# Forget-gate sums and step-width softplus issued beside projection steps in a hybrid streaming encoder step

## The chip, the cores and the metric

The kernel runs on one core of one Trainium2 chip. The metric is the device time of one execution in microseconds. The core has five engines that run side by side and wait for each other through semaphores: PE (matrix products), DVE (vector work), ACT (activation functions and copies), POOL (further element-wise work) and SP, which issues the DMAs here. PE writes to PSUM banks, and ACT or DVE must read a bank out before PE may fill it again.

## The reference

One layer of a trunk is computed for 1024 frames of a new stream and for 16 frames of each of 8 running streams, 1152 rows in all. Three mixers work on the same normalised input: a stick-breaking attention (4 heads), a forgetting attention "FoX" (4 heads) and a state-space scan "SSD" (8 heads). One input projection feeds all three.

```python
proj = jnp.einsum('bnd,de->bne', u, p['w_in'])
sq, sk, sv, fq, fk, fv, fg, z, xbc, dt = split_last(proj, IN_SIZES)
logf = jax.nn.log_sigmoid((fg + p['fox_b_f']).astype(jnp.float32))
fcum = jnp.cumsum(logf, axis=1)                      # running sum of the forget gates
fox_o = query_sweep(lambda qb, fb, qp: fox_attend(qb, fk, fv, fb, fcum, qp, kpos), (fq, fcum), n)
xbc_c = jax.nn.silu(causal_dwconv(xbc_pad, p['conv_w'], p['conv_b']))
dt = jax.nn.softplus((dt + p['dt_bias']).astype(jnp.float32))   # the step widths
y, h_final = ssd_scan(xs * dt[..., None], dt * A, Bm, Cm, h0, ssd_chunk)
```

For the running streams the sums of the gates start from 1024 cached gate values of each stream. After the mixers come an output projection, a cross-attention and a SwiGLU feed-forward net.

## The kernel before

All products are in split precision: an operand is stored as a rounded part (hi) and a remainder (lo), and each product is three matmuls (function `mm3`, lines L328 to L330). Weights are loaded by SP into `wr` tiles (4 buffers), ACT casts the hi part into `wh` (L292) and POOL subtracts to get the lo part `wl` (L132, in pieces of at most 256 columns). The same `wr`, `wh` and `wl` buffers also hold the cached keys and values of the running streams.

The middle of the program interleaves two generators. The **main** one is `pipeline`: 112 steps of attention, first the stick-breaking heads (`m = 0`), then the FoX heads (`m = 1`). A step is a block of 128 query rows (scores L561/L562, mask L564, then for `m = 0` two sigmoids on ACT L518/L519, a running product on DVE L521 and a product on POOL L132), or the product of finished weights with the values (transposes L579, ACT copies L582, products L594). In between are four decode units per mixer, each for two running streams: their rows load cached keys (L886), transpose them (L892, copies L894), and score them (L877, L905, L906); their value step is L928, L937 and L960.

The **fill** is a second generator, from which the loop takes one step per attention step (`RATE[0]` = 1.0). It is `fill_s`: projections of FoX queries and keys in 12 steps, of FoX values and gates in 9 (`proj_v(1)`; the gates go to tile `lf`), then `fox_sums` in 4 steps and `pad_cols`, then, in the order of `ORD`, the first half of z with the step widths in 9 steps (`z_proj(0)`; widths go to tile `dts`), `dt_softplus` in 1, the eight convolution blocks `xbc` in 24, and the second half of z in 9. A projection step is one output tile: 24 matmuls for a z block, in one PSUM bank of the pool `psd`, which has 2 banks. When `fill_s` ends, the SSD generator `ssd_gen` (51 steps) takes its place at 1.1 steps per attention step. What is left of it when attention ends runs between the steps of the output projection.

`fox_sums` and `dt_softplus` have no projection in them. Each turns gates into log form by a chain of small ACT and DVE instructions (`log1p_exp_negabs`, L402 to L412). `fox_sums` then makes running sums by small products (L686, L687, L694, L709 to L711, L729, each with a `psd` bank), scans (L700) and DMAs to and from DRAM. A z block's bank is read three times before it is free: by ACT for the tanh and by DVE for the gate (`gate`, L417 and L418) and for the step widths (L804).

The order on each engine is not written out: a scheduler places the instructions by their order of issue as priority and by its own model of time. Each engine then runs its queue strictly in that order, so an instruction that waits also holds up all behind it.

Of the kernel before, what the change touches and what calls it, by code (L numbers as in the profile page):

```python
# [62 lines left out]
def tile_hybrid_step(ctx: ExitStack, tc: tile.TileContext, a: dict):  # L63
# [34 lines left out]
    def xc_t(dt=F32):  # L98
        return xcp.tile([P, 1056], dt, tag="xc", name="xc")
# [10 lines left out]
    def pd():  # L110
        return ps_t(psd, "d")
# [230 lines left out]
    def dense_T(w, uc, jobs):  # L342


        units = [(w_unit([(w, c0, P)], 0, KT), f) for c0, f in jobs]
        for c in range(NCH):
            for (wh, wl), consume in units:
                ps = pd()
                uh, ul = uc[c]
                for k in range(KT):  # L350
                    mm3(ps[:, :CW], wh[:, k, :], wl[:, k, :], uh[:, k, :], ul[:, k, :], k == 0, k == KT - 1)
                later = consume(c, ps[:, :CW])
                flush()
                if later:
                    late.append(later)
                yield
# [4 lines left out]
    def flush():  # L361
        if late:
            late.pop()()

    def dense_N(srcs, ub, consume):

        n = sum(s[2] for s in srcs)
        u0 = w_unit(srcs, 0, 4)
        u1 = w_unit(srcs, 4, 4)
        for blk, (uh, ul) in enumerate(ub):  # L370
            ps = pd()
            for k in range(KT):
                wh, wl = (u0, u1)[k // 4]
                mm3(ps[:, :n], uh[:, k, :], ul[:, k, :], wh[:, k % 4, :], wl[:, k % 4, :],
                    k == 0, k == KT - 1)
            consume(blk, ps[:, :n])
            yield

    def blocks_of(uc):
        return [(uc[b // 3][0][:, :, (b % 3) * P:(b % 3 + 1) * P],  # L380
                 uc[b // 3][1][:, :, (b % 3) * P:(b % 3 + 1) * P]) for b in range(NBLK)]
# [38 lines left out]
    def drain(g):  # L420
        for _ in g:
            pass
# [361 lines left out]
    def pad_cols():  # L784
        sct = xc_t()[0:24, :D]
        SP.dma_start(out=sct, in_=a["state_conv"][0].rearrange("b i c -> (b i) c"))
        tp = pd()
        for j in range(8):
            PE.transpose(tp[:, 24 * j:24 * j + 24], sct[:, j * P:(j + 1) * P], ident[:24, :24])
        DVE.tensor_copy(pads, tp[:, :192].rearrange("p (j b i) -> p j b i", j=8, i=3))  # L790

    def xbc_proj(j0, j1):
        for j in range(j0, j1):
            yield from dense_T(w_in, uc, [xbc_job(j)])
        flush()


    def consume_z(n):
        def f(blk, ps):
            t, zt = sg2_t(), sg_t()  # L800
            gate(zt[:, :256], ps[:, :256], t, 0.5)
            SP.dma_start(out=z_sc[blk * P:(blk + 1) * P, n * 256:(n + 1) * 256], in_=zt[:, :256])
            if n == 0:
                DVE.tensor_tensor(out=dts[:, blk, :], in0=ps[:, 256:264], in1=hb[:, 4:12], op=ALU.add)  # L804
        return f

    def z_proj(n):
        yield from dense_N([(w_in, C_Z + 256 * n, 256)] + [(w_in, C_DT, 8)] * (n == 0), blocks_of(uc), consume_z(n))

    def dt_softplus():  # L810
        l = log1p_exp_negabs(dts, [P, NBLK, 8])
        DVE.scalar_tensor_tensor(dts.rearrange("p a b -> p (a b)"), dts.rearrange("p a b -> p (a b)"), 0.0,
                                 l.rearrange("p a b -> p (a b)"), ALU.max, ALU.add)
# [414 lines left out]
    aux = chunks((0, 1, 2))  # L1228
# [5 lines left out]
    drain(dense_T(w_in, uc, [(C_SK + P, consume_qk(3, 1, None, p_k[0], s_k[0]))]))  # L1234
    drain(proj_v(0, C_SV, p_v[0], s_v[0]))

    def fill_s():
        yield from dense_T(w_in, uc, [(C_FQ, consume_qk(4, 0, QS))])
        yield from dense_T(w_in, uc, [(C_FQ + P, consume_qk(5, 1, QS))])
        yield from dense_T(w_in, uc, [(C_FK, consume_qk(6, 0, None, p_k[1], s_k[1]))])  # L1240
        yield from dense_T(w_in, uc, [(C_FK + P, consume_qk(7, 1, None, p_k[1], s_k[1]))])
        yield from proj_v(1, C_FV, p_v[1], s_v[1], extra=4)
        yield from fox_sums()
        pad_cols()
        for o in ORD:
            if o == "z1":

                for hd in range(4):
                    tc.keep_in_program_order(
                        SP.dma_start(out=fs4.rearrange("(b h) i k -> b h i k", h=4)[:, hd],  # L1250
                                     in_=fs_sc[hd].unsqueeze(1).to_broadcast([DEC_B, 4, PAST])))
                for p in range(4):
                    tc.keep_in_program_order(
                        SP.dma_start(out=fqs[:, p:p + 1], in_=fn_sc[8 * p:8 * p + 8, :]))
            if o[0] == "z":
                yield from z_proj(int(o[1]))
            elif o == "dt":
                dt_softplus()
                yield
            else:  # L1260
                yield from xbc_proj(*o)

    def mixed(m, at, fc, nxt):

# [22 lines left out]
    u0, _ = mixed(0, AT0, None, load1)  # L1287
# [747 lines left out]
```

## Time and profile before

| | |
|---|---|
| time, median of 3 runs | 1906.57 us (1905.22 to 1914.69) |
| span of the profiled execution | 1911.2 us |
| its own time | not listed apart from the span |
| PE busy | 1834.5 us, 96% of the span |
| DVE, ACT, POOL busy | 894.3, 822.7, 627.9 us |

The profile is of one execution. Its span alone is 4.6 us above the median of the runs, 0.24%, so it stands among the slower ones. In the views, "x" is a count, a bracket gives the idle time before an instruction and what ended it, and PEclk is the clock that PE was granted, 1.00 being full speed. Matmuls overlap, so PE's busy time counts covered time. The profile calls L521 and L700 scans by their own name; the listings of the order call them SCALAR_TENSOR_TENSOR.

### The profile page before, as it was taken

The numbers are of one execution on the slowest core, as the hardware profiler recorded it, in microseconds if no ns is written. First come the engines' busy times: TensorE is split into PE (matmuls) and PEld (weight loads), VectorE is DVE, ScalarE is ACT, GpSimd is POOL, SyncE is SP. The second block draws the span as 40 slices with busy tenths as digits, with TensorE's granted clock in tenths as the row PEclk, the third lists the DMA queues.
The fourth block names the chain that finished last, engine by engine and source line by source line (L and its number), as shares of the span: only waits on it lengthen the run. The fifth ranks groups of instructions, "written<-read, shape, count | busy, mean of one in ns | idle before, by whom it ended". The sixth has DMA issues, their size and how long they took to land.

```text
span 1911.2 us, 32463 instructions
## 1 busy us (share of the span) xinstructions
PE 1834.5 (96%) x12120; PEld 1637.6 (86%) x12120; DVE 894.3 (47%) x1823; ACT 822.7 (43%) x1779; POOL 627.9 (33%) x923
## 2 busy tenths in 40 slices
PE   7989988999998899999999999999999999999998
PEld 5889876888876677899998889999999999788886
DVE  3421323557656882354444487333333333455554
ACT  6531543535666870344343275333333333344443
POOL 7632416254224662211112105454444542000000
PEclk9999998999999999999999999999999999999999
DMA  9455645536579896345567124223322223566672
GB/s 338 141 165 159 207 139 129 161 102 186 174 237 291 268 323 217 111 144 162 180 210 270 61 83 119 70 71 81 88 73 70 70 70 104 188 196 228 183 245 91
DMA packets 302365, 306.07 MB, mean 160 GB/s; under 512 B 82428, under 2 KB 253668, under 8 KB 302208
## 3 DMA queue, kind: packets, MB, share of 16 engines
q1 hardware_dynamic: 302208, 304.01, 51.4%
q8 instruction: 95, 1.56, 0.3%
q14 instruction: 62, 0.51, 0.1%
HBM read 229.84 MB, written 74.63 MB: 159 GB/s over the span
## 4 chain that ended last, share of the span: by engine, by line
PE 81%; DMA 6%; DVE 3%; POOL 3%; issue 3%; ACT 2%; SPq 1%; POOLq 0%; DVEq 0%; ACTq 0%
PE psd L1857 11%; PE psd L328 10%; PE psd L329 10%; PE psd L330 9%; PE pst L1857 8%; PE pss L1857 4%; PE pss L328 3%; PE pss L329 3%; PE pss L330 3%; PE pso L1857 2%; PE pso L594 2%; PE pst L328 1%; PE pst L329 1%; PE pst L330 1%; POOL wl L132 1%
## 5 line engine op out<-in xcount | busy, mean ns | idle before, releaser
L132 POOL TENSOR_TENSOR wl<-wr,wh 128x256 fp32r<-128x256 f32 (+2 forms) x184 | 140.9, 800 | 219.4 <-ACT wh L292 215.7
L328 PE MATMUL psd<-act,wh 128*128 128x384 f32 x576 | 199.2, 346 | 4.8 <-DVE sg L455 2.7
L329 PE MATMUL psd<-act,wh 128*128 128x384 f32 x576 | 197.9, 344 | 0.0
L330 PE MATMUL psd<-act,wl 128*128 128x384 f32 x576 | 197.1, 342 | 0.0
L1857 PE MATMUL pst<-bT,tr 128*128 128x256 f32 (+1 forms) x1068 | 155.0, 293 | 0.0
L1857 PEld LDWEIGHTS pst<-bT,tr 128*128 128x128 f32 x1068 | 144.9, 188 | 0.1
L328 PE MATMUL psd<-wh,act 128*128 128x256 f32 (+3 forms) x414 | 133.7, 326 | 3.4 <-DMA act<-osc 1.5
L330 PE MATMUL psd<-wh,act 128*128 128x512 f32 (+3 forms) x424 | 136.6, 323 | 0.0
L329 PE MATMUL psd<-wl,act 128*128 128x256 f32 (+3 forms) x414 | 133.7, 324 | 0.0
L1857 PE MATMUL psd<-bT,tr 128*128 128x320 f32 (+1 forms) x912 | 132.9, 295 | 0.8 <-DVE tr L1701 0.5
L1857 PEld LDWEIGHTS psd<-bT,tr 128*128 128x128 f32 x912 | 124.7, 188 | 1.3 <-DVE tr L1701 0.7
L328 PEld LDWEIGHTS psd<-act,wh 128*128 128x128 f32 x576 | 109.3, 190 | 8.4 <-DVE sg L455 3.1
L132 POOL TENSOR_TENSOR tr<-u,tr 128x256 fp32r<-128x256 f32 x110 | 82.6, 780 | 100.2 <-ACT tr L1697 82.2
L329 PEld LDWEIGHTS psd<-act,wh 128*128 128x128 f32 x576 | 109.5, 190 | 1.5 <-issue 1.1
L330 PEld LDWEIGHTS psd<-act,wl 128*128 128x128 f32 x576 | 109.2, 190 | 1.3 <-issue 1.0
L132 POOL TENSOR_TENSOR ws<-ws 128x256 f32<-128x256 f32 (+2 forms) x100 | 70.1, 729 | 115.1 <-DVE ws L521 102.4
L253 POOL TENSOR_SCALAR sm<-sm 128x1 f32<-128x1 f32 (+2 forms) x27 | 8.3, 308 | 299.0 <-ACT y L1940 210.7
L1832 DVE TENSOR_TENSOR tr<-tr,pst 128x256 f32<-128x256 f32 (+1 forms) x86 | 38.6, 449 | 138.3 <-ACT tr L1829 105.1
L132 POOL TENSOR_TENSOR tr<-raw,tr 128x256 fp32r<-128x256 f32 x94 | 69.4, 767 | 85.6 <-ACT tr L1697 77.5
L1697 ACT CAST tr<-tr 128x384 fp32r<-128x384 f32 (+1 forms) x70 | 37.7, 538 | 121.4 <-DMA tr<-hidsc 119.0
L328 PEld LDWEIGHTS psd<-wh,act 128*128 128x128 f32 x414 | 79.2, 192 | 11.6 <-issue 1.8
L292 ACT CAST wh<-wr 128x512 fp32r<-128x512 f32 (+2 forms) x90 | 52.2, 621 | 80.9 <-PE psd L330 31.0
(622 smaller groups left out, 4697.9 us busy)
## 6 DMA issues: line engine op xcount, KB each, us to landing
u<-w_down SPq DMA_DIRECT2D x40, 512.0 KB
raw<-w_down SPq DMA_DIRECT2D x26, 512.0 KB
st<-qksc SPq DMA_DIRECT2D x48, 256.0 KB
wr<-w_in SPq DMA_DIRECT2D x44, 256.0 KB
tr<-hidsc SPq DMA_DIRECT2D x57, 192.0 KB
hidsc<-tr SPq DMA_DIRECT2D x34, 288.0 KB
qksc<-sg SPq DMA_DIRECT2D x48, 192.0 KB
wr<-cache_sb_k SPq DMA_DIRECT2D x32, 256.0 KB
```

What stands on the lines that cost most here:

```text
L132: POOL.tensor_tensor(out=out[:, a0:a1], in0=in0[:, a0:a1], in1=in1[:, a0:a1], op=op)
L253: POOL.tensor_scalar(v, ss, inv, EPS, ALU.mult, ALU.add)
L292: ACT.copy(hi, raw)
L328: PE.matmul(out, ah, bh, start=start, stop=False)
L329: PE.matmul(out, ah, bl, start=False, stop=False)
L330: PE.matmul(out, al, bh, start=False, stop=stop)
L594: return PE.matmul(po[r:r + 64, q_], vt[:, 2 * (k0 + i) + j, :], pfs[i][:, sl], start=start and k0 == 0 and (j == 0 or qp > 0), stop=k0 + ...
L1697: ACT.copy(hi, src)
L1832: DVE.tensor_tensor(out=at(out, g), in0=at(x, g), in1=ps[g][:, :GW[g]], op=op)
L1857: PE.matmul(dst[g][:, :GW[g]], x[:, ka], y[:, k, :], start=start and k == 0 and m == 0, stop=stop and k == 3 and m == 2, skip_group_check= ...
```

## The change

The four steps of `fox_sums` and the one of `dt_softplus` no longer take a step of the fill. A helper `beside` draws one step of a second generator after each step of a projection, before the projection's step ends. `fox_sums` and `pad_cols` so run with the blocks 1 to 5 of `z_proj(0)`, and `dt_softplus` with the second tile of the first `xbc` block. The fill has 63 projection steps then, where it had 68 steps with 63 projections among them.

```diff
+    def beside(main, aux):
+        for _ in main:
+            next(aux, None)
+            yield
+        drain(aux)
+    def sums():
+        yield
+        yield from fox_sums()
+        pad_cols()
+    def steps():
+        yield
+        dt_softplus()
     def fill_s():
...
         yield from proj_v(1, C_FV, p_v[1], s_v[1], extra=4)
-        yield from fox_sums()
-        pad_cols()
         for o in ORD:
...
-            if o[0] == "z":
-                yield from z_proj(int(o[1]))
+            if o == "z0":
+                yield from beside(z_proj(0), sums())
+            elif o == "z1":
+                yield from z_proj(1)
             elif o == "dt":
-                dt_softplus()
-                yield
+                continue
             else:
-                yield from xbc_proj(*o)
+                yield from beside(xbc_proj(*o), steps())
```

No instruction is added or taken away on any engine; only their order changes. Three places show it.

On **PE**, behind the last block of the FoX value projection (matmuls of 260 columns), the kernel before has the key transposes and scores of the second decode unit (L892, L877), with the first product of the sums (L686) among transposes of attention weights (L579):

```order
L330 MATMUL psd<-wh,act 128x260
L892 MATMUL pst<-ident,wr 128x128 x16
L877 MATMUL pss<-kf,st 32x512 x4
L892 MATMUL pst<-ident,wr 128x128 x13
L579 MATMUL pst<-ident,ws 128x128 x4
L892 MATMUL pst<-ident,wr 128x128 x3
L579 MATMUL pst<-ident,ws 128x128 x4
L686 MATMUL psd<-lf,sg 128x32
```

In the changed kernel, with the z blocks (matmuls of 264 columns) cut to their first rows, the same place reads:

```order
L330 MATMUL psd<-wh,act 128x260
L328 MATMUL psd<-wh,act 128x264
...
L892 MATMUL pst<-ident,wr 128x128 x2
...
L892 MATMUL pst<-ident,wr 128x128 x6
...
L892 MATMUL pst<-ident,wr 128x128 x4
...
L892 MATMUL pst<-ident,wr 128x128 x12
L877 MATMUL pss<-kf,st 32x512 x4
L892 MATMUL pst<-ident,wr 128x128 x8
L579 MATMUL pst<-ident,ws 128x128 x8
L877 MATMUL pss<-kf,st 32x512 x4
```

The first two z blocks (48 matmuls) have moved in front of and between the first 24 key transposes, and the third stands behind the second L877, around L686 and L687. The rows left out are matmuls of these two blocks. Their weights move too: their loads (L317) and casts (L292), which stood among the decode unit's instructions, now stand ahead of the last value block's.

On **DVE**, in the same stretch of the changed kernel, the running products of the attention rows (L521) and the instructions that free a PSUM bank (L688 copies a result of the sums, L418 and L804 read the third z block's bank) stand in this order:

```order
L521 SCALAR_TENSOR_TENSOR ws<-ws 128x1152
L688 COPY fqc<-psd 128x32
L521 SCALAR_TENSOR_TENSOR ws<-ws 128x896
L604 TENSOR_TENSOR so<-pso,so 64x256
L452 TENSOR_TENSOR sg<-so,sg 64x256
L521 SCALAR_TENSOR_TENSOR ws<-ws 128x1024
L418 SCALAR_TENSOR_TENSOR sg<-so,psd 128x256
L804 TENSOR_TENSOR dts<-psd,hb 128x8
```

The third z block's bank is freed only behind three running products; before the change no z block was in flight here.

On **PE**, where the last block of the second z half ends and the SSD generator begins (L1005 is its first product), the kernel before has all key transposes of the first FoX decode unit behind it. The changed kernel has 15 of the 32 still ahead, among the first SSD transposes (L1018, L1058, L1132):

```order
L1005 MATMUL psd<-act 128x64
L1006 MATMUL psd<-act 128x8
L1007 MATMUL psd<-act 128x64
L1008 MATMUL psd<-act 128x8
L594 MATMUL pso<-pt,st 64x256 x3
L594 MATMUL pso<-pt,st 64x128
L1010 MATMUL psd<-act 128x8 x4
L892 MATMUL pst<-ident,wr 128x128 x11
L1018 MATMUL psd<-ident,act 72x128
L1058 MATMUL psd<-ident,act 128x128 x4
L892 MATMUL pst<-ident,wr 128x128 x4
L1132 MATMUL pst<-ident,act 128x128 x4
```

What moved is that FoX attention steps 64 to 68, which ran beside z blocks, now run beside the first five SSD steps; the listing starts where the z blocks are over.

## The prediction

> **What bounds the kernel now.** I read the page first: the span, the busy times and the chain of work that ended last.
>
> ```profile
> span 1911.2 us, 32463 instructions
> ...
> PE 1834.5 (96%) x12120; PEld 1637.6 (86%) x12120; DVE 894.3 (47%) x1823; ACT 822.7 (43%) x1779; POOL 627.9 (33%) x923
> ...
> PE 81%; DMA 6%; DVE 3%; POOL 3%; issue 3%; ACT 2%; SPq 1%; POOLq 0%; DVEq 0%; ACTq 0%
> ```
>
> PE is busy for 96% of the span and carries 81% of the chain. No instruction is added or removed, so PE's work stays, and the change can only move the 77 us in which PE is idle and the time in which its clock is low. Next I read the busy times by stretches of 5 us around the four steps of the sums. Columns: stretch in us, its length, busy time of PE, PE's weight loads, DVE, ACT and POOL with counts, PE's clock, DMA share, GB/s.
>
> ```profile
> 275.00:280.00 5.00, 3.31 (x27) 1.88 (x25) 2.58 (x12) 3.90 (x11) 1.69 (x3) 1.00 0.63 204
> 280.00:285.00 5.00, 3.01 (x25) 2.45 (x24) 3.63 (x20) 2.83 (x6) 1.38 (x4) 1.00 0.87 233
> 285.00:290.00 5.00, 4.57 (x40) 2.36 (x40) 0.19 (x1) 3.35 (x7) 4.59 (x9) 1.00 0.80 113
> 290.00:295.00 5.00, 2.36 (x14) 1.29 (x12) 2.33 (x1) 3.17 (x9) 2.58 (x3) 1.00 0.84 202
> 295.00:300.00 5.00, 1.72 (x8) 1.10 (x7) 4.97 (x9) 3.67 (x9) 5.00 (x5) 0.51 1.09 259
> 300.00:305.00 5.00, 3.42 (x18) 3.26 (x19) 1.91 (x4) 0.98 (x3) 5.00 (x7) 0.50 0.56 153
> 305.00:310.00 5.00, 5.00 (x29) 5.00 (x29) 1.23 (x3) 1.15 (x3) 4.88 (x13) 0.63 0.11 26
> ```
>
> The stretch lies between the last block of the value projection and the first z block, which begins at 306.33 (row below). Between 275 and 310 PE is idle for 1.69 + 1.99 + 0.43 + 2.64 + 3.28 + 1.58 = **11.6 us**, and from 295 to 310 its clock is about half: the busy time there, 1.72 at 0.51, 3.42 at 0.50 and 5.00 at 0.63, contains 0.84 + 1.71 + 1.85 = **4.4 us** that full speed would not have taken. The hole is worth **16.0 us**. The timeline says what PE stands for (start, duration, engine, line; a bracket is idle time and its end):
>
> ```profile
> 278.35 1.05 SPq L886 DMA_DIRECT2D wr<-cache_sb_k  x2
> 282.73 1.00 PE L892 MATMUL pst<-ident,wr 128*128 128x128 f32 x5 [1.90 <-DMA wr<-cache_sb_k]
> 291.83 0.63 ACT L292 CAST wh<-wr 128x528 fp32r<-128x528 f32 x1 [3.48 <-DMA wr<-w_in]
> 292.37 0.27 ACT L518 ACTIVATE ws<-pss 128x128 f32<-128x128 f32 x1
> 292.54 5.56 POOL L132 TENSOR_TENSOR wl<-wr,wh 128x256 fp32r<-128x256 f32 x3 [2.42 <-ACT wh L292]
> 292.67 3.01 DVE L521 TENSOR_TENSOR_SCAN ws<-ws 128x1152 f32<-128x1152 f32 x1 [3.55 <-ACT ws L518]
> 292.86 0.44 PE L561 MATMUL pss<-st 128*128 128x384 f32 x1 [2.54 <-ACT ws L519]
> 296.00 2.08 DVE L521 TENSOR_TENSOR_SCAN ws<-ws 128x896 f32<-128x896 f32 x1
> 296.23 0.60 ACT L518 ACTIVATE ws<-pss 128x512 f32<-128x512 f32 x1
> 298.81 2.27 DVE L521 TENSOR_TENSOR_SCAN ws<-ws 128x1024 f32<-128x1024 f32 x1
> 301.57 1.13 PE L928 MATMUL pst<-ident,ws 128*128 128x128 f32 x4 [4.38 <-POOL ws L132]
> ```
>
> Two chains lie here, and neither is the arithmetic of the sums. First, the cached keys of the decode unit: two loads are issued at 278.35 and PE gets them at 282.73, after 1.90 idle. Second, the decode row's chain. ACT stands for 3.48 us for the weights of the coming z block (L292), so the last sigmoid of the row (L518, 128 columns) starts at 292.37 only. Then come the running product (3.01), POOL, which is busy with the z weights for 5.56, and the transposes L928, which find PE idle for 4.38. The sums are beside all this; what they lack is a projection that fills PE meanwhile. Wider stretches show what a filled stage looks like (same columns):
>
> ```profile
> 309.00:350.00 41.00, 39.18 (x357) 35.08 (x357) 11.23 (x26) 14.59 (x37) 11.71 (x19) 1.00 0.36 106
> 350.00:361.00 11.00, 11.00 (x77) 9.84 (x75) 5.22 (x20) 4.60 (x11) 0.21 (x1) 1.00 0.49 134
> 361.00:546.30 185.30, 181.76 (x1320) 162.09 (x1319) 114.23 (x196) 100.81 (x228) 76.50 (x111) 0.99 0.62 179
> 546.30:712.00 165.70, 148.17 (x1188) 112.08 (x1186) 124.12 (x365) 120.73 (x275) 89.56 (x142) 0.99 0.84 274
> 712.00:731.00 19.00, 15.95 (x138) 11.96 (x136) 7.36 (x17) 3.01 (x7) 9.81 (x16) 1.00 0.90 292
> ```
>
> From 309 to 350, attention beside z blocks, PE is idle for 1.82 of 41 us; from 361 to 546.3, beside `xbc` and z, for 3.5 of 185.3. From 546.3 to 712, attention beside the SSD steps, it is idle for **17.5** of 165.7 us, although no other engine is busier than 124. I call that the lean stage.
>
> **The change part by part.**
>
> *The hole, what goes.* Two z blocks now stand before and among the key transposes. The price of a block is in the second and third of these rows:
>
> ```profile
> 306.33 0.57 PE L328 MATMUL psd<-wh,act 128*128 128x264 f32 x1
> 309.68 0.28 PE L328 MATMUL psd<-wh,act 128*128 128x264 f32 x1
> 309.80 0.28 PE L329 MATMUL psd<-wl,act 128*128 128x264 f32 x1
> 287.48 1.08 PE L594 MATMUL pso<-pt,st 128*64 128x256 f32 x8
> ```
>
> A z matmul starts 0.12 us after the one before it, so a block of 24 costs 2.9 us and the two cost 5.8 us, against waits of 1.90 us for keys. The z weights are loaded ahead of the last value block, so ACT's 3.48 us and POOL's 5.56 us no longer lie in the decode row's chain. 16.0 us is the most that goes.
>
> *The hole, what stays.* (a) The last eight key transposes have only twelve others and one score group in front of them (listing), some 2.4 us, while the load took from 279.40, the end of its issue, to 282.73. I take 1.2 us; the ends are 0 and the 1.90 seen. (b) The third z block's bank is released on DVE only behind three running products, and with two banks in `psd`, which the sums need too, the fourth block must wait for one. That chain is 2 x 0.27 for the sigmoids of 128 columns, 3.01, 2.08, four sigmoids of 0.60 and 2.27: 10.3 us. PE has about 6.8 us for it, estimated from these rows: one block of 2.9, values products of 1.08 and about half as much again, and five or six score pieces whose first matmul is 0.44. I take 3.5 us left; the ends are 0 and the 7.5 us that PE idled from 290 to 305. (c) The clock. I take 2.0 us, between 0 and the 4.4 seen, since a gap of two or three us stays likely under (b). Together 6.7 us stay (0 to 13.8), and **9.3 us** go (2.2 to 16.0; that the same work loses more with more cover beside it is excluded here, and late keys elsewhere are the third rival).
>
> For the clock the rows are these, the stretches of 1 us around its two falls:
>
> ```profile
> 294.00:295.00 1.00, 0.90 (x5) 0.60 (x4) 1.00 (x1) 1.00 (x4) 1.00 (x1) 1.00 0.98 213
> 295.00:296.00 1.00, 0.53 (x6) 0.41 (x5) 1.00 (x3) 0.98 (x4) 1.00 (x1) 0.53 1.08 246
> 564.68 2.07 PE L1136 MATMUL psd<-sg,act 128*128 128x256 f32 x4 [1.88 <-ACT sg L1134]
> 565.00:566.00 1.00, 1.00 (x3) 0.82 (x3) 1.00 (x3) 1.00 (x4) 0.00 (x0) 0.50 0.08 16
> ```
>
> It fell at 295 after a gap of 2.54 us (292.86 above), and at 565 after one of 1.88. The Trainium skill, "TensorE: Matmul & The Clock Gate", section "HAM oscillation — how this bites in real kernels", gives as its abstract rule that there be no PE gaps above about 3.4 us; both falls here came after shorter ones, so the trace disagrees and the measurement decides. By the page's rule term (c) would be 0 and the forecast 2.0 us lower.
>
> *The width's softplus.* Its step ran from 350.6 to 356.8:
>
> ```profile
> L402 ACT ACTIVATE sg<-dts x1: 263/263/263, 350.6 to 350.6; 128x72 f32<-128x72 f32 x1
> L812 DVE SCALAR_TENSOR_TENSOR dts<-dts,sg x1: 234/234/234, 356.6 to 356.6; 128x72 f32<-128x72 f32 x1
> ```
>
> From 350 to 361 PE was busy 11.00 of 11.00. So dropping this step saves 0: the cover is the z block before it and the `xbc` block behind. Beside an `xbc` tile it is covered in the same way; without cover it would cost up to its 6.2 us.
>
> *Five attention steps more in the lean stage.* The fill has 63 projection steps instead of 68, so the SSD steps begin five attention steps sooner (64 instead of 69 of 112), and the lean stage holds 49 steps instead of 44. Steps 64 to 68 contain a FoX decode unit. The three such units that were in the lean stage waited so (wait, total us, times, longest):
>
> ```profile
> PE pst L892 <- DMA wr<-cache_fox_k: 3.1, 2, 2.0
> PE pss L877 <- DVE sm L535: 1.3, 2, 0.7
> PE pst L892 <- ACT kf L894: 0.8, 1, 0.8
> ```
>
> That is 5.2 us, 1.7 for a unit. The other 41 steps share 17.5 - 5.2 = 12.3 us, 0.3 each. One unit and four steps: 1.7 + 1.2 = 2.9, and 0.2 for the clock: **3.1 us** come back. The lower end is 0, for steps beside projections cost next to nothing (1.82 in 41 us); the upper is 8.5: the 4.1 us of the first three rows of the hole, keys without cover, and one fall of the clock at 4.4.
>
> *The end of attention.* Counting steps, 48 of the 51 SSD steps were done when attention ended, and three ran beside the output projection; now all 51 are done two steps early. From 712 to 731 PE was idle 3.05 us. The three steps no longer hold banks there, but no SSD product covers the last attention rows either. I take 0, with -3 and +3 as ends.
>
> Sum: -9.3 + 0 + 3.1 + 0 = **-6.2 us**. The profile's own time is not given beside its span, and its span is 4.6 us above the median, so I take the sum off the median: 1906.57 - 6.2 = 1900.4.
>
> **The rivals.**
>
> *Nearly all of the hole goes.* If the scheduler's mix of z and attention works here as from 309 to 350, 1.8 us in 41, then 1.5 us stay of the 16.0 in its 35 us. For it: that stage has the same parts, a decode value step included. Against it: the three running products ahead of L418. -14.5 + 3.1 = -11.4, or 1895.2.
>
> *The change doesn't do what it says: the hole only moves.* Five attention steps lose their projections wherever they stand. If steps 64 to 68 lose what the four steps and a decode unit lost at 275 to 310, less what SSD products cover, and that is the 9.3 us won, the time is 1906.6. For it: a decode unit is among the five, and DMA is busy at a share of 0.84 through the lean stage. Against it: the lean stage's 0.3 us a step.
>
> *Slower: the decode keys come late at the start of the SSD stage.* Its place is the third listing: 15 key transposes stand ahead of the first SSD transposes, and PE can pass none of them. Their loads share SP's queue with the eight state loads (L1182), of which four held that queue for 5.64 us:
>
> ```profile
> 533.41 5.64 SPq L1182 DMA_DIRECT2D act<-state_ssm  x4
> ```
>
> If the last keys are queued behind these and land later than the end of the last z block, which decides, PE stands with no projection left: the hole's 16.0 again and the 5.64 of the queue. 16.0 + 5.6 - 9.3 = +12.3, or 1918.9. For it: DMA share 0.84, and 3.1 us of key waits there already. Against it: z blocks of 2.9 us each run while these loads are issued.
>
> **How the numbers follow.** Forecast 0.46, nearly all gone 0.26, only moved 0.17, slower 0.11. About 0.5%, 9.5 us, is what a measurement of this kernel can tell from no change. Below 1897.0 lie most of the second case (0.22) and the forecast's low end (0.06): 0.28. Above 1916.1 lies nearly all of the last: 0.10. The rest is 0.62. The term's ends added up would give -19 and +9; the range leaves out the last case and the corners in which all ends meet: 1890 to 1914.
>
> **What would show it.** In the changed profile: right if PE's idle between the last value block and the fourth z block is 3 to 7 us; wrong at 10 or more, or at 2. Right on (b) if the z blocks wait for L418 or for a copy behind the running products. PEclk below 1 for less than 5 us there. PE idle around the softplus near 0. In the lean stage idle of 19 to 22 us, with L892 waiting for DMA at its start for under 3; above 28 the third rival holds. What would make it all wrong is a shift in places that no step names: the scheduler reorders the whole middle, and a few us may come or go in `xbc`.

## The result, and the profile after

The changed kernel is **slower by 0.6%**: 1922.71 us (median of 6 runs, 1918.40 to 1930.38) against 1912.51 us for the kernel before in the same set of runs (6 runs, 1905.22 to 1916.74); the ratio is 1.006, 95% interval 1.0041 to 1.0079. The forecast was 1900.4, range 1890 to 1914: 6.2 us off a median of 1906.57 us. Over six runs that median is 5.9 us higher, so 5.9 of the 22.3 us between forecast and time belong to the base; the change itself was forecast at -6.2 us and measured at +10.2. The profiled execution took 1918.4 us, 1.7 us more than its span; it is the fastest of the six, so its trace shows only part of the loss: its span is 5.5 us above the profiled span before. That one, 1911.2 us against a median time of 1912.51, turns out to lie near the middle of the six runs, not among the slower ones.

From the page after, the same three lines as before:

```profile
span 1916.7 us, 32477 instructions
...
PE 1840.2 (96%) x12120; PEld 1641.7 (86%) x12120; DVE 893.3 (47%) x1823; ACT 822.6 (43%) x1779; POOL 624.7 (33%) x923
...
PE 44%; DVE 1%; DMA 1%; issue 0%; ACT 0%; POOL 0%; SPq 0%; DVEq 0%; POOLq 0%; ACTq 0%
```

The chain of the changed kernel, followed back from the end, breaks off near 1009 us (its shares add up to 46%), so it says nothing of the stages below. The 14 instructions more are semaphore events.

PE's busy time has grown by 5.7 us for the same 12120 matmuls, and its idle time is the same to 0.3 us (76.5, before 76.7). So no idle time was won in sum, and PE was busy longer for the same work.

The wins and losses show by stages. Two views of busy time by stretches follow, first before, then after. Columns: stretch, length, busy time and count of PE, PE's weight loads, DVE, ACT and POOL, PE's clock, DMA share, GB/s. The stretches are: last value block to the last block of the first z half; `xbc` and the second z half; SSD beside attention, up to the end of attention; the rest of the SSD steps and the output projection.

```profile
274.50:349.30 74.80, 61.36 (x500) 51.22 (x499) 28.33 (x73) 33.34 (x79) 36.09 (x54) 0.91 0.52 137
349.30:546.70 197.40, 193.86 (x1402) 173.02 (x1401) 119.45 (x216) 105.90 (x240) 76.89 (x113) 0.99 0.61 176
546.70:714.50 167.80, 150.27 (x1257) 113.68 (x1256) 125.91 (x369) 121.48 (x276) 90.19 (x144) 0.99 0.84 276
714.50:770.60 56.10, 52.97 (x238) 42.05 (x239) 17.69 (x30) 7.81 (x16) 18.58 (x28) 1.00 0.62 199
```

The changed kernel, the same stretches of work:

```profile
276.20:334.30 58.10, 52.41 (x460) 44.56 (x458) 26.10 (x69) 27.72 (x67) 26.54 (x46) 1.00 0.54 149
334.30:528.60 194.30, 189.75 (x1356) 171.21 (x1355) 117.93 (x207) 99.58 (x230) 79.53 (x111) 0.99 0.56 165
528.60:728.20 199.60, 175.89 (x1385) 131.99 (x1383) 132.79 (x392) 132.85 (x297) 95.51 (x154) 0.96 0.81 259
728.20:777.50 49.30, 46.83 (x199) 37.39 (x197) 12.46 (x20) 6.63 (x13) 15.03 (x22) 0.97 0.58 196
```

In the first stretch PE was idle for 13.4 us at a clock of 0.91, and is now for 5.7 us at 1.00. In the third it was idle for 17.5 us at 0.99, and is now for 23.7 at 0.96. Below, the **loss** of a stretch is PE's idle time plus busy time times (1 - clock), summed over pieces of 0.5 us of the trace. By stretches it went from 17.8 to 5.7, from 5.3 to 6.3, **from 19.2 to 31.7**, and from 3.1 to 4.1 us. The rest of the program, whose order the change hardly touches, loses 1.0 us less. These sum to +1.3 us. The other 4.2 us of the span are PE busy time at full clock. If each matmul is counted from its start to the next one's start or its own end, times the clock, the transposes of 128x128 (L579, L892 and others) take 5.6 us more than before and all other matmuls 1.5 us less. A matmul that stands alone counts for all its length, while one in a row overlaps its neighbours, so this is likely the same transposes in shorter rows; that is inferred.

The hole by stretches of 5 us, as it was shown of before:

```profile
275.00:280.00 5.00, 5.00 (x44) 5.00 (x43) 2.93 (x4) 3.40 (x7) 4.20 (x7) 1.00 0.27 81
280.00:285.00 5.00, 4.54 (x39) 4.30 (x37) 0.90 (x4) 2.05 (x6) 1.41 (x3) 1.00 0.81 262
285.00:290.00 5.00, 3.96 (x32) 2.29 (x34) 2.50 (x12) 3.35 (x8) 1.36 (x4) 1.00 0.85 241
290.00:295.00 5.00, 4.13 (x38) 2.35 (x37) 3.45 (x18) 2.22 (x6) 0.00 (x0) 1.00 0.48 108
295.00:300.00 5.00, 5.00 (x38) 4.26 (x37) 2.09 (x3) 2.35 (x6) 2.84 (x6) 1.00 0.67 140
300.00:305.00 5.00, 3.24 (x21) 2.47 (x20) 3.20 (x4) 4.88 (x12) 3.23 (x6) 1.00 1.08 238
305.00:310.00 5.00, 5.00 (x41) 4.75 (x40) 4.63 (x10) 1.38 (x6) 4.88 (x9) 1.00 0.26 65
```

PE's idle time from 275 to 310 is now 0 + 0.46 + 1.04 + 0.87 + 0 + 1.76 + 0 = 4.1 us (11.6 before), and its clock does not fall.

The SSD stage, in the timeline of the changed kernel where the first FoX decode unit meets the first SSD steps (start, duration, engine, line; a bracket is idle time and its end):

```profile
521.91 3.78 SPq L1182 DMA_DIRECT2D act<-state_ssm  x5
532.04 0.34 SPq L886 DMA_DIRECT2D wr<-cache_fox_k  x1
532.75 0.63 PE L892 MATMUL pst<-ident,wr 128*128 128x128 f32 x4 [0.80 <-ACT kf L894]
533.87 0.63 PE L892 MATMUL pst<-ident,wr 128*128 128x128 f32 x4 [0.50 <-DMA wr<-cache_fox_k]
535.19 0.34 SPq L886 DMA_DIRECT2D wr<-cache_fox_k  x1
538.65 0.63 PE L892 MATMUL pst<-ident,wr 128*128 128x128 f32 x4 [3.01 <-DMA wr<-cache_fox_k]
```

The second z half ended at 528.6. PE now stands for cached keys: 0.80 us for the copy of an earlier tile (L894), 0.50 and 3.01 for loads. The last load was issued at 535.19, long after the state loads had left SP's queue (525.7), between transposes of the tiles that are loaded before it. In the second place, 40 us later, an SSD load holds up attention through ACT:

```profile
572.79 0.57 SPq L1043 DMA_DIRECT2D act<-acsc  x1
577.73 0.98 ACT L1081 ACTIVATE act<-act 128x128 f32<-128x128 f32 x3 [8.05 <-DMA act<-acsc]
579.76 0.46 ACT L582 COPY pt<-pst 128x384 f32<-128x384 f32 x1
580.27 1.54 PE L594 MATMUL pso<-pt,st 128*64 128x256 f32 x4 [3.50 <-ACT pt L582]
```

SP issued the decay sums of the first prompt block at 572.79. ACT's exponentials (L1081) stand in its queue ahead of a copy of attention weights (L582) and waited 8.05 us for them; PE's value product (L594) waited 3.50 us for that copy.

### The profile page after: what moved, and what is told of

It is laid out like the page before. It is cut to its first block, busy times and chain, and to the rows that moved or that the text cites. A ratio compares the mean times of both kernels' runs of the same rounds, so it can differ in the third digit from the quotient of the medians.

```text
span 1916.7 us, 32477 instructions
## 1 busy us (share of the span) xinstructions
PE 1840.2 (96%) x12120; PEld 1641.7 (86%) x12120; DVE 893.3 (47%) x1823; ACT 822.6 (43%) x1779; POOL 624.7 (33%) x923
## 5 line engine op out<-in xcount | busy, mean ns | idle before, releaser
L132 POOL TENSOR_TENSOR wl<-wr,wh 128x256 fp32r<-128x256 f32 (+2 forms) x184 | 135.9, 773 | 268.0 <-ACT wh L292 266.9
L329 PEld LDWEIGHTS psd<-wl,act 128*128 128x128 f32 x414 | 79.1, 191 | 8.7 <-issue 2.0
```

What stands on the lines that cost most here:

```text
L132: POOL.tensor_tensor(out=out[:, a0:a1], in0=in0[:, a0:a1], in1=in1[:, a0:a1], op=op)
L329: PE.matmul(out, ah, bl, start=False, stop=False)
```

## The experiments

The loss is explained in different ways. **A**: the hole is won, some 10 us, and given back because the SSD stage starts five attention steps sooner. **B**: an attention step with no projection beside it costs about 2 us wherever it stands. **C**, later sharpened to **F**: what counts is which SSD steps meet which attention steps in the order, and there is no simple rule. **D**: the SSD's weights steps (exponentials on ACT and DVE) cost where they meet row steps of attention. **E**: the cost is the two places shown above. **G**: the later the SSD starts, the better.

Each ratio is against the kernel before, run on the same chip in the same set (medians there 1912.5 to 1914.9). The last columns are the loss in us of one profiled execution, as defined above, for the first z half, `xbc` with the second z half, and the SSD stage. In the first 160 us, where all twenty kernels have the same order on PE, that loss lies between 19.6 and 24.5 us, so a difference of some 5 us between two profiles decides nothing. There is no e15.

| kernel | sums | SSD from step | SSD steps per step | ratio (95%) | z | xbc, z | SSD |
|---|---|---|---|---|---|---|---|
| before | own | 69 | 1.1 | 1 | 17.8 | 5.3 | 19.2 |
| the change | beside | 64 | 1.1 | 1.006 (1.0041 to 1.0079) | 5.7 | 6.3 | 31.7 |
| e1 | beside | 65 | 1.1 | 1.0114 (1.009 to 1.0139) | 5.9 | 7.0 | 41.5 |
| e2 | own | 68 | 1.1 | 1.0088 (1.0064 to 1.0112) | 15.3 | 10.3 | 30.4 |
| e3 | beside | 69 | 1.1 | 1.0006 (0.9994 to 1.0019) | 6.0 | 11.7 | 22.5 |
| e4 | own | 64 | 1.1 | 1.0193 (1.0173 to 1.0213) | 18.6 | 10.2 | 51.2 |
| e5 | beside | 64 | 1.1, held | 1.0046 (1.003 to 1.0063) | 6.1 | 7.3 | 38.9 |
| e6 | own | 69 | 1.1, held | 1.0009 (0.9994 to 1.0024) | 16.7 | 4.9 | 20.0 |
| e7 | beside | 64 | 1.1 | 1.0085 (1.0054 to 1.0116) | 5.6 | 6.0 | 41.0 |
| e8 | beside | 64 | 1.1 | 1.011 (1.0081 to 1.0139) | 8.7 | 6.1 | 43.7 |
| e9 | beside | 69 | 1.1 | 0.9999 (0.998 to 1.0017) | 6.6 | 14.5 | 23.6 |
| e10 | own | 70 | 1.1 | 1.006 (1.004 to 1.008) | 16.8 | 9.4 | 25.1 |
| e11 | own | 67 | 1.1 | 1.0022 (1.0002 to 1.0042) | 15.6 | 4.1 | 29.8 |
| e12 | beside | 64 | 1.0 | 0.9999 (0.9983 to 1.0016) | 6.0 | 5.4 | 30.6 |
| e13 | beside | 64 | 1.0 | 1.0059 (1.0038 to 1.008) | 7.0 | 5.0 | 32.9 |
| e14 | beside | 64 | 1.0 | 1.0013 (0.9999 to 1.0027) | 8.5 | 5.1 | 33.6 |
| e16 | beside | 64 | 0.9 | 1.0047 (1.003 to 1.0064) | 6.4 | 7.2 | 35.0 |
| e17 | own | 69 | 1.0 | 1.0065 (1.0046 to 1.0083) | 19.0 | 4.9 | 28.6 |
| e18 | beside | 69 | 1.1 | 1.0015 (1.0 to 1.0031) | 6.3 | 5.5 | 39.4 |
| e19 | beside | 69 | 1.1 | 1.004 (1.0025 to 1.0054) | 14.1 | 4.8 | 24.2 |

### e3 and e4: the hole and the start of the SSD apart

e3 puts five bare steps among the `xbc` blocks of the changed kernel; e4 takes five steps out of the kernel before.

```diff
+    def spread(main):                     # e3
+        for n, _ in enumerate(main):
+            yield
+            if n in (5, 8, 11, 14, 17):
+                yield
...
-                yield from beside(xbc_proj(*o), steps())
+                yield from spread(beside(xbc_proj(*o), steps()))
```

```diff
+    def merged(main):                     # e4
+        for n, _ in enumerate(main):
+            if n not in (5, 8, 11, 14, 17):
+                yield
...
-                yield from xbc_proj(*o)
+                yield from merged(xbc_proj(*o))
```

> The change, with five attention steps without any projection put in among the xbc blocks (one after each of five xbc tiles), so that the second half of z stands again beside steps 60 to 68 and the SSD steps begin at step 69, as before the change; the sums and the width's softplus stay beside projections. Theory A (the hole is won, about 10 us, and lost again because the SSD stage begins five attention steps sooner): the gain shows, 0.994 to 0.997 of the kernel before, with PE idle of 1 to 4 us more between 310 and 550 us and 19 to 22 us from the last z block to the output projection. Theory B (an attention step without a projection beside it costs its 2 us wherever it stands): 1.002 to 1.007, as the change itself, with the idle time now among the xbc blocks. Theory C (chance meetings of decode units and SSD steps, not their number): as A here.

> The kernel before, sums and softplus still as steps of their own, with five xbc chunks each put into the step of the chunk before it, so that the second half of z stands beside steps 55 to 63 and the SSD steps begin at step 64, as in the change. Theory A: the loss alone, without the gain: 1.007 to 1.011 of the kernel before; idle of 10 to 12 us in the four steps of the sums as before, and 25 us or more with three or more falls of the clock from the last z block to the output projection. Theory B: 0.998 to 1.002, since no attention step loses its cover but those of the sums, which had lost it already, and the ones at the end. Theory C: as A.

Measured: 1.0006 and 1.0193. The busy time by stretches of e3, for the first z half, `xbc` with the second z half, and the SSD stage (columns: stretch, length, PE busy, clock, DMA share, GB/s):

```profile
279.00:337.10 58.10, 53.69 (x459) 0.97 0.54 149
337.10:548.00 210.90, 202.58 (x1442) 0.98 0.59 169
548.00:719.00 171.00, 151.65 (x1257) 0.98 0.83 270
```

The hole stays won (loss 6.0), and from the first SSD product on e3 has the very order of PE instructions of before; its SSD stage loses 22.5 us where the same order lost 19.2. But the five bare steps lose 11.7 us among the `xbc` blocks, against 5.3. The ratio lies between the ranges of A and B. A is right that the hole is won and that the stage loses less in its old place, and B on where most of the gain of e3 went: 11.8 won, 6.5 given back by the bare steps (3.3 more in the SSD stage is within what two profiles of the same work differ by). e4 has the loss alone, and twice as much as A expected.

### e1 and e2: each half of the change alone

```diff
-                continue                                       # e1: sums beside, softplus a step
+                dt_softplus()
+                yield
...
-                yield from beside(xbc_proj(*o), steps())
+                yield from xbc_proj(*o)
...
+        yield from fox_sums()                                  # e2: softplus beside, sums four steps
+        pad_cols()
...
-                yield from beside(z_proj(0), sums())
+                yield from z_proj(0)
```

> The sums beside z blocks, the width's softplus a step of its own as before: the SSD steps begin at step 65. Theory A: gain of 10 us, loss of four fifths of some 16 us: 1.000 to 1.003 of the kernel before. Theory B: 1.000 to 1.006. Theory C: one step's difference against the change can decide which SSD step meets the first FoX decode unit; anywhere from 0.995 to 1.008, and the waits of 3.0 us for cached keys and 3.5 us for the copies of the transposed weights in the changed kernel are gone or elsewhere.

> The width's softplus beside an xbc chunk, the sums four steps of their own as before: the SSD steps begin at step 68. Theory A: no gain, a fifth of the loss: 1.001 to 1.003 of the kernel before. Theory B: 0.999 to 1.002. Theory C: anywhere from 0.998 to 1.008.

Measured: 1.0114 and 1.0088. e2 takes out one step, the softplus's, so that `xbc`, the second z half and the SSD all come one attention step earlier. Its SSD stage loses 30.4 us for 19.2, and the stage ahead of it 10.3 for 5.3. Both ratios lie above all that was expected, C's upper end of 1.008 included; C is the only theory that has large effects of single steps at all.

### e5 and e6: the weights steps

The pipeline tells whether its step is a value step, the SSD generator tells whether its next step is a weights step, and the loop holds that step back (e5 on the change; e6, with `not av`, on the kernel before).

```diff
-    for k, _ in enumerate(pipeline(u0, LAG0, u1, LAG1)):
+    held = False
+    for av in pipeline(u0, LAG0, u1, LAG1):
...
-        while acc >= 1.0:
+        while acc >= 1.0 and (av or not held):
             with hp("ssd" if done[0] else "dense"):
-                next(fill, None)
+                held = next(fill, None)
```

> The change, with every weights step of the SSD (the exponentials on ACT and DVE, eight of them after the first) held back until an attention step that multiplies by the values, where before the change six of eight stood and in the changed kernel two of eight; the steps behind it catch up there. Theory D (the SSD stage loses where its weights steps, heavy on ACT and DVE, meet the row steps of attention, which are heavy on them too): idle and clock loss from the last z block to the output projection falls from 31.7 us to 18 to 24, 0.994 to 1.000 of the kernel before. Theory E (the loss is at two places at the start of the stage: the FoX keys, and the late load of the first prompt block's decay sums): these two places stay, 1.003 to 1.007. Theory F (it is the order's chance, no single rule): anywhere from 0.996 to 1.012.

> The kernel before, with every weights step of the SSD held back until a row step of attention (scores and softmax), where before two of eight stood. Theory D: the stage's loss grows from 19.2 us to 30 or more, 1.005 to 1.012. Theory E: 0.998 to 1.003, as the keys and the first load are where they were. Theory F: 0.998 to 1.012.

Measured: 1.0046 with all eight on value steps, 1.0009 with seven on row steps and one left over. Both speak against D: its good meeting leaves 38.9 us of loss (in the slowest of ten executions), and its bad one costs nothing. But these are steps of issue, and the scheduler followed them in part only. In e6 every engine has its instructions in the order of the kernel before up to 627 us, 80 us into the stage; in e5 all have the order of the change up to 583 us, 54 us into it. So D is tested in the rest of the stage alone.

### e7 and e8: the two places by themselves

```diff
-AT0, AT1 = (3, 7, 11, 15), (4, 8, 12, 16)
+AT0, AT1 = (3, 7, 11, 15), (3, 8, 12, 16)      # e7
...
         weights(order[0], A, B)
+        nxt = load(order[1])                   # e8
         yield
```

> The change, with the first FoX decode unit one attention unit earlier (three steps), so that its sixteen key transposes stand beside z blocks again and not ahead of the first SSD transposes. Theory E and my third rival: the waits of 0.8, 0.5 and 3.0 us at 532 to 539 us and the fall of the clock behind them go, 0.996 to 1.000 by the first place alone 1.002 to 1.003. Theory D: what the shift does to the weights steps decides (their attention steps stay nearly the same), 1.002 to 1.005. Theory F: 0.996 to 1.012.

> The change, with the load of the first prompt block of the SSD (xbc, decay sums and gate) issued behind the decode block's weights instead of ten steps later. Theory E: the 8.05 us in which ACT stands for the decay sums at 577.7 us, the 3.5 us of PE behind it and the fall of the clock there go, some 5 us: 1.003 of the kernel before. Theory D: 1.003 to 1.006, since the other meetings stay. Theory F: 0.996 to 1.012.

Measured: 1.0085 and 1.011, both slower than the change. In e7 PE no longer waits for keys at the start of the stage (it waits 3.15 us for those of the next unit, at 590.42). In e8 ACT no longer waits for the decay sums of the first prompt block. The SSD stage by stretches, cut at the ends of the four FoX value products of decode units, first the change, then e8 (columns as for e3):

```profile
528.60:573.00 44.40, 39.69 (x306) 0.96 0.63 201
573.00:633.00 60.00, 49.33 (x368) 0.90 0.80 249
633.00:679.00 46.00, 42.76 (x365) 0.98 0.88 288
679.00:728.20 49.20, 44.12 (x357) 1.00 0.91 296
```

The same stretches of work in e8:

```profile
532.30:586.00 53.70, 45.42 (x315) 0.90 0.69 210
586.00:634.00 48.00, 42.20 (x366) 1.00 0.85 262
634.00:691.00 57.00, 44.08 (x356) 0.91 0.73 233
691.00:742.60 51.60, 44.04 (x365) 0.93 0.84 282
```

In the second stretch, which holds the second place, PE's idle time falls from 10.67 to 5.80 us and the clock returns to 1.00. But the third goes from 3.24 to 12.92 us idle, the first from 4.71 to 8.28. In the third it is the same wait again, at a later prompt block:

```profile
641.54 0.99 ACT L1081 ACTIVATE act<-act 128x128 f32<-128x128 f32 x3 [8.00 <-DMA act<-acsc]
643.86 2.04 PE L1098 MATMUL psd<-act 128*128 128x256 f32 x4 [6.52 <-DVE so L452]
```

DVE's L452 works on what ACT's cast L451 gives it, and that cast stands in ACT's queue right behind the exponentials. Two more such waits of ACT follow, 4.00 us at 657.19 and 7.28 at 697.6, with 3.17 and 4.74 us of PE behind them. ACT stands for decay sums for 19.9 us in e8, 8.05 in the change. So E is right on what the waits do; e8 moved one load, and the wait moved to other blocks. Whether the loads of all blocks, issued earlier, would gain was not tried. The time that ACT waits for decay sums doesn't order the losses by itself: it is 13.1 us in the kernel before, 5.8 in e16 and 28.5 in e4.

### e9 to e12: thin cover, the start, the rate

e9 spreads five `xbc` chunks over two attention steps each in place of e3's bare steps. e10 does this with one chunk of the kernel before; e11 merges two of its chunks as e4 does with five. e12 sets the rate to 1.0 in the changed kernel.

```diff
-    def dense_T(w, uc, jobs):
+    def dense_T(w, uc, jobs, halved=()):          # e9, e10
...
                     mm3(ps[:, :CW], wh[:, k, :], wl[:, k, :], uh[:, k, :], ul[:, k, :], k == 0, k == KT - 1)
+                    if k == 3 and c in halved:
+                        yield
...
-            yield from dense_T(w_in, uc, [xbc_job(j)])
+            yield from dense_T(w_in, uc, [xbc_job(j)], (2,) if j in (1, 2, 3, 4, 5) else ())
...
-RATE = (1.0, 1.1, 60)
+RATE = (1.0, 1.0, 60)                             # e12
```

> The change, with five of the 24 xbc chunks spread over two attention steps each (four of eight products in each), so that no attention step is bare and the SSD steps begin at step 69 again, as before the change. If what the bare steps cost (idle and clock loss from the xbc blocks to the last z block 11.7 us, against 5.3 before the change) was their lack of any projection, it falls to 5 to 8 us, the stage behind keeps its 19 to 23 us, and the gain of the hole remains: 0.994 to 0.999 of the kernel before. If thinner cover costs the same as bare steps (theory B, the projections are only moved): 0.999 to 1.003.

> The kernel before, with one xbc chunk spread over two steps: SSD steps from step 70 instead of 69, nothing else. Theory F (69 is one good meeting of two sequences, and any other start loses): 1.004 to 1.010, with 0.6 us or more of idle and clock loss to each attention step of the SSD stage, where it is 0.44 before. Theory G (each attention step that passes from the SSD stage to the projections gains; the later the start, the better): 0.996 to 1.000, 0.35 to 0.45 us a step.

> The kernel before, with two xbc chunks each put into the step of the chunk before: SSD steps from step 67, the sums as before. Theory F: anywhere from 1.002 to 1.015, not in order with the starts at 68 (1.009) and 64 (1.019). Theory G: in order between them, 1.010 to 1.014.

> The change, with one SSD step for each attention step instead of 1.1, so that two of the 51 are left for the output projection (three before the change, none in it) and no attention step has two. If the doubled steps or the two bare attention steps at the end make the loss: idle and clock loss of the SSD stage 20 to 25 us, 0.997 to 1.001. Theory F: 1.002 to 1.012. Theory G: as the change, 1.004 to 1.008.

Measured: 0.9999, 1.006, 1.0022 and 0.9999. Half a chunk beside a step is no better than none (loss of 14.5 us among `xbc` and z), as B has it. A start one step later than before (e10) loses as one a step earlier does (4.1 us of it beside `xbc` and z, where its split chunk is, 5.9 in the SSD stage), and a start at 67 loses less than one at 68: G falls. F stands, but its ranges were so wide, 0.996 to 1.012 in e5 to e8, that this says little, and e12 lies below the 1.002 where its range began. e12 ties with the kernel before; in its profiled execution the SSD stage still loses 30.6 us, close to the change, so where it is better than the change isn't shown by one profile of each.

### e13 to e17: the two places and the rate once more

e13 is e12 with the load of e8, e14 is e12 with the decode unit of e7. e16 sets the rate of the change to 0.9, e17 that of the kernel before to 1.0.

> The change with one SSD step for each attention step, and the load of the first prompt block ahead (behind the decode block's weights). Theory E in a good order: the 3.6 us at 581 us, 3.4 of clock there go, 0.997 to 0.999 of the kernel before. Theory F: 0.996 to 1.010, with new waits at other places whatever becomes of this one.

> The change with one SSD step for each attention step, and the first FoX decode unit one attention unit earlier. Theory E in a good order: the 3.3 us at 539 us and the fall of the clock behind go, 0.997 to 0.999 of the kernel before. Theory F: 0.996 to 1.010, with new waits at other places.

> The change with 0.9 SSD steps for each attention step, which leaves seven of the 51 for the output projection. If the rate has a trend (the fewer SSD steps meet attention, the less is lost): 0.994 to 0.999 of the kernel before, and less than 28 us of idle and clock loss in the SSD stage. Theory F: 0.998 to 1.010, out of order with 1.006 at a rate of 1.1 and 1.000 at 1.0.

> The kernel before with one SSD step for each attention step, which leaves seven of the 51 for the output projection. If the rate itself is what helped the change: 0.994 to 0.998. Theory F: the good meeting from step 69 is spoilt, 1.002 to 1.010.

Measured: 1.0059, 1.0013, 1.0047 and 1.0065. Neither removal gains on e12. On the changed kernel the rates 1.1, 1.0 and 0.9 give 1.006, 1.000 and 1.005, no trend; on the kernel before 1.0 loses.

### e18 and e19: thin cover at other places

e18 spreads five blocks of the second z half over two steps each, e19 five of the twelve chunks of FoX queries and keys, both as e9 does.

> The change, with five of the nine blocks of the second half of z spread over two attention steps each, so that the SSD steps begin at step 69. If FoX steps, which have no running product, get by with thin cover: 0.995 to 0.999 of the kernel before. Theory B: 0.999 to 1.003, with 9 us or more of loss in that half of z. Theory F: up to 1.010, since the order from the SSD start on is not that of before.

> The change, with five of the twelve q and k chunks at the start of attention spread over two attention steps each, so that the value projection, the z blocks with the sums, xbc, z and the SSD steps (from step 69) come later by five steps; from the SSD start on PE's instructions have the same order as before the change. If thin cover costs by its place: less than 3 us more from the start to the first z block, the hole's gain of 10 to 12 us remains, the SSD stage keeps 19 to 23 us: 0.994 to 0.997 of the kernel before. Theory B (five steps cost what the hole cost, wherever they stand): 0.999 to 1.003.

Measured: 1.0015 and 1.004. In e18 the scheduler still put the first SSD product near where the change has it (530.3 us, 528.6 in the change), so its thin cover was not tried as meant. e19 has the order of before from the first SSD product on, and its SSD stage loses 24.2 us. But the stretch from 206 us to the end of the value projection now loses 12.5 us (5.7 in the change), 11.7 of them ahead of the first value block, beside the last of the q and k steps, and the sums, which meet other attention steps, make PE wait beside z. In e19's timeline, L688 is the first product of the sums (L686 in the kernel before), and L664 the end of their log chain on DVE (L662):

```profile
325.27 0.61 PE L688 MATMUL psd<-lf,sg 128*128 128x32 f32 x2 [6.09 <-DVE lf L664]
```

So five attention steps without their projection, or with half of it, cost something in each of three kernels: 6.5 us more than before in e3, 9.2 in e9, and here, with what it did to the sums, 12.5 + 14.1 - 5.7 - 5.7 = 15.2 more than in the change.

No kernel of the set beats the kernel before.

## Why the prediction was wrong

**The hole: right, and a little too low.** I had 9.3 of 16.0 us going and 3 to 7 us of idle time left; 4.1 us of idle time are left and the clock holds, so 11.9 went. Of the parts that stay, (a) the keys cost 0.56 us (1.2 forecast) and (c) the clock nothing (2.0). For (b), no z block waited for L418: PE's other waits are 0.81 us for a copy of keys, 0.87 for the sums' own chain (L686), 0.53 for a load and 1.23 for scores behind a sigmoid (L519). So the mechanism of (b) was wrong, and that the idle time left lies in my 3 to 7 us is in part luck. The gain holds in other orders: with the sums as steps of their own the first z stretch loses 15.3 to 19.0 us in seven kernels, with the sums beside it 5.6 to 8.7 in twelve. e19, where the sums met other attention steps, shows that cover alone doesn't guarantee it (14.1).

**The softplus: right for what was priced.** It now runs from 343.0 to 350.8 us, and PE is busy for 8.00 of the 8.00 us from 343 to 351, so dropping its step could save nothing there. What I didn't see is that the step, whatever it holds, also sets where all behind it starts. e2 drops only this step and costs 0.9%.

**Five steps more in the lean stage: the step that failed.** I took 0.3 us for an attention step and 1.7 for a decode unit from the averages of the stage before, and 0.2 for the clock, 3.1 us in all, at most 8.5. The stage's loss grew by 12.5 us: 6.2 of idle time, 6.3 of clock. The sum treats the stage as the old one with five average steps added. It is another one: each of its SSD steps meets another attention step, and PE, ACT and DVE have another order. The runs show how much that matters. The kernels that keep PE's old order in it (before, e3, e19, and e9 from 2 us behind its start) lose 19.2 to 24.2 us, and e6, which keeps it for half, 20.0. All others lose 25.1 to 51.2 us; per attention step that is 0.44 (before) to 1.05 (e4). Even one step's shift, with 45 steps instead of 44, took 11.2 us more. My upper end came from adding prices of single waits, and no such price bounds what a new order does.

**The clock there: left out almost wholly.** I had seen one fall in the old stage and wrote down 0.2 us (the two falls that I showed are not all of the middle: the old trace has another at 400.88 us, beside `xbc`). The new stage has four falls. Three come with waits of 2 us or more that end at 538.65, 580.27 (both shown) and 630.34 (2.01 us). The other begins at 597.30, in the middle of a wait of 1.84 us that ends at 598.18, and lasts two periods of 3.41 us.

**The third rival: right place, wrong mechanism.** The late keys are there, at the start of the SSD stage, without a projection to cover them. But they cost PE 0.80 + 0.50 + 3.01 us and one fall of the clock, at most 1.7, some 6 us and not 21.6, and the state loads were no longer in the queue. I infer from the timeline that the loads waited for the four buffers, since they were issued as transposes freed them; only e7, which moved the unit and so removed the wait, bears on it. The rest of the loss is elsewhere in the stage. That its price, 1918.9, came near the time is chance.

**The rival that the hole only moves** came nearest in kind. I spoke against it with the 0.3 us a step. What five attention steps without their projection lose (6.5 us in e3, 9.2 in e9) is most of what the hole gives. I had given it a chance of 0.17 and a price of no change.

**The end of attention: right.** The last steps and the output projection lose 4.1 us for 3.1.

**My tests**: idle of the lean stage 19 to 22 us, above 28 for the third rival, and under 3 us of L892 waiting for loads at its start. The idle time came to 23.7 to the end of attention, which by that test speaks for no rival, and L892's waits to 3.5. A test on idle time alone misses what the clock takes.

What stays open is why the order from step 69 at 1.1 is better than its neighbours. The weights steps (e5, e6, as far as they moved), the two waits taken singly (e7, e8, e13, e14) and a trend in the start or the rate (e10, e11, e12, e16, e17) don't explain it. That it is the sum of many small meetings is not shown, and late loads at every block of the stage stay as an untested rival.

## What to carry to other kernels

A step in an interleaving has two costs: what it does, and where it puts all that follows. Before pricing the first, test the second by itself: shift what follows by one step (e2, e10 here: +0.9% and +0.6%), and don't forecast a gain that is smaller than such a shift costs. A wait that is removed at one place of a densely shared stage can come back at the next, as the decay sums' did in e8, so judge an edit by the loss of the whole stage, the clock included, and not by the wait that it removed.

## What the runs showed of the hardware

PE's clock falls by a rule that the traces of all twenty kernels bear out, with few exceptions. The clock's record changes only at multiples of 3.41 us from its first entry. Over all such periods in which the clock was full, I compared PE's idle time in one period with the clock of the next. Under 1.2 us of idle time, 3 of 10487 were followed by half clock; from 1.2 to 1.8 us 42 of 188; from 1.8 us on 151 of 154. Busy time by stretches of the changed kernel, two pairs of one period and the next (columns as for e3):

```profile
484.70:488.11 3.41, 1.28 (x16) 1.00 0.32 101
488.11:491.53 3.42, 3.42 (x72) 0.51 0.20 60
535.90:539.31 3.41, 0.66 (x6) 1.00 1.08 311
539.31:542.72 3.41, 3.41 (x18) 0.50 1.03 398
```

A pair of the kernel before:

```profile
639.80:643.21 3.41, 1.65 (x13) 1.00 0.85 302
643.21:646.62 3.41, 3.41 (x21) 1.00 1.02 333
```

2.13 us idle (3.41 - 1.28) and 2.75 us (3.41 - 0.66) are followed by a clock of 0.5; 1.76 us (3.41 - 1.65) is not. So a wait need not be long to cost twice: about half a period is enough, in one piece or several, and the next 3.41 us then run at half clock, worth up to 1.7 us. A wait that lies across the border of two periods mostly costs only itself: of 39 waits of 1.8 us or more that left less than 1.8 us of idle time in each of the two periods, 32 were followed by no fall. The seven others include the fall at 295 of the kernel before and the one at 597.30 of the change, which is also one of the three under 1.2 us. The Trainium skill, "TensorE: Matmul & The Clock Gate", section "What's actually happening", has a free-running window of 3413 ns, which the rows agree with. Its section "HAM oscillation — how this bites in real kernels" has gaps of over about 3.4 us as the abstract rule; here half of that did it.
